# Nearest-neighbour upsampling by two: each store's copy shared between VectorE and ScalarE

## The chip, the cores and the metric

The kernel runs on one core of a Trainium2 chip. The metric is the device time of one execution in microseconds; of a kernel the median of its runs is given.

A core has several engines with instruction queues of their own. Three matter here: VectorE (DVE in the profile) and ScalarE (ACT), which can copy data within the on-chip memory, and SyncE (SP), which issues DMA transfers. ScalarE can issue DMA transfers too, so there are two DMA queues, one fed by SP (q1 in the profile) and one by ScalarE (q10). Both are served by the core's 16 DMA engines.

## What is computed

```python
def setup_inputs():
    batch, channels, h, w = (16, 64, 64, 64)
    return {'x': np.random.randn(batch, channels, h, w).astype(np.float32), 'scale_factor': 2}

def reference(x, scale_factor):
    ...
    for i in range(new_h):
        for j in range(new_w):
            result[:, :, i, j] = x[:, :, i // scale_factor, j // scale_factor]
    return result
```

The input is 16 x 64 images of 64 x 64 float32, 16.78 MB. Each element goes to a 2 x 2 block of the output, so the output is four times as large, 67.11 MB. There is no arithmetic.

## The kernel before

All 65536 image rows are laid over 128 partitions, R = 512 rows of 64 elements for each. A row becomes two output rows of 128 elements, 256 elements in all, and the 256 elements lie next to each other in the output. So a partition's part of the output is one contiguous stretch, and a store of k rows writes k x 1024 bytes for each partition.

Everything on the chip lives in one tile, `mem`. Its upper part, `xt`, from element WF = 79 x 256 = 20224 on, takes the whole input, 512 x 64 elements. The part below is free space for expanded rows. Three loads on SP bring the input: rows 0 to 31, 32 to 287 and 288 to 511 (`HEAD`, `cuts`, L192 to L195). They are issued ahead of the barrier at the start of the program (`begin_before_barrier`).

Then nine steps follow, n = 0 to 8, with 54, 38, 54, 60, 54, 62, 64, 62 and 64 rows (`rows`, L181). In a step a copy expands k rows into a region `u` of `mem` and a store sends the region to the output. The copy's source is `expanded(r0, r1)` (L197), the rows of `xt` with each row repeated twice and each element repeated twice. The regions alternate. Even steps use the bottom of `mem`, from element 0. Odd steps use the stretch that ends where the rows of this step begin, `at = WF + r0 * W - size`; so they overwrite input rows that earlier steps have already expanded. A copy must wait until the store that last used any of its elements has landed, which in most steps is the store two steps before.

All copies run on VectorE. In step 0 there are two, one for row 0 (L214), which needs the first load alone, and one for the other 53 (L215). The other steps have one each. The stores of steps 0, 1 and 8 are issued by SP, and those of steps 2 to 7 by ScalarE, whose queue holds nothing else. At the end `close_early` arranges that all engines but SP and GpSimd are finished early, and that SP's last instruction waits for the last store alone.

Below, "copy n" and "store n" are those of step n.

Of the kernel before, what the change touches and what calls it, by code (L numbers as in the profile page):

```python
# [153 lines left out]
@with_exitstack  # L154
def kernel(
    ctx: ExitStack,
    tc: tile.TileContext,
    x: bass.AP,
    scale_factor: int,
    out: bass.AP,  # L160
):
    nc = tc.nc
    nc.at_finalize(begin_before_barrier)
    nc.at_finalize(close_early)
    P = nc.NUM_PARTITIONS
    s = int(scale_factor)
    B, C, H, W = x.shape
    R = B * C * H // P
    fdt = x.dtype

    xp = x.rearrange("b c h w -> (b c h) w").rearrange("(p r) w -> p r w", p=P)
    op = out.rearrange("b c (h hd) w -> (b c h) (hd w)", hd=s).rearrange(
        "(p r) w -> p r w", p=P
    )

    rows = [54, 38, 54, 60, 54, 62, 64, 62, 64]  # L181
    GROW = s * s
    FREE = 79
    WF = FREE * GROW * W
    assert sum(rows) == R
    mem_pool = ctx.enter_context(tc.tile_pool(name="mem", bufs=1))
    mem = mem_pool.tile([P, WF + R * W], fdt, name="mem")
    xt = mem[:, WF:].rearrange("p (r w) -> p r w", r=R)

    HEAD = 32  # L192
    cuts = [0, HEAD, R // 2 + HEAD, R]
    for lo, hi in zip(cuts, cuts[1:]):
        nc.sync.dma_start(out=xt[:, lo:hi], in_=xp[:, lo:hi])  # L195

    def expanded(r0, r1):  # L197
        return (
            xt[:, r0:r1].unsqueeze(2).unsqueeze(4).to_broadcast([P, r1 - r0, s, W, s])
        )  # L200

    r0 = 0
    before = (0, 0)
    for n, k in enumerate(rows):
        size = k * GROW * W
        at = 0 if n % 2 == 0 else WF + r0 * W - size
        assert at >= before[1] or at + size <= before[0]
        before = (at, at + size)
        u = mem[:, at : at + size].rearrange(
            "p (k a w b) -> p k a w b", k=k, a=s, w=W  # L210
        )
        k0 = 1 if n == 0 else 0
        if k0:
            nc.vector.tensor_copy(out=u[:, :k0], in_=expanded(r0, r0 + k0))  # L214
        nc.vector.tensor_copy(out=u[:, k0:], in_=expanded(r0 + k0, r0 + k))  # L215
        issuer = nc.sync if n in (0, 1, len(rows) - 1) else nc.scalar
        issuer.dma_start(out=op[:, r0 : r0 + k, :], in_=u)
        r0 += k
# [35 lines left out]
```

## Time and profile before

| what | value |
|---|---|
| median of three runs | 197.15 us (197.02 to 197.16) |
| the profiled execution, its own time | 197.01 us |
| span in the profile, first to last instruction | 195.7 us |
| read from and written to HBM | 16.78 MB and 67.11 MB, 429 GB/s over the span |
| the three loads land at | 4.86, 24.2 and 41.1 us |
| store 0 issued, landed | 38.5, 57.5 us |
| store 8 issued, landed | 166.4, 195.7 us |
| issue of a store to its landing, least, median, most | 18.9, 26.5, 36.7 us |

The span is the time from the first to the last instruction that the profile shows; some 1.3 us of the execution lie around it. DVE is VectorE, ACT ScalarE, SP SyncE; ACTq and SPq are their DMA queues. L215 is line 215 of the kernel. A group such as `mem<-mem 128x13824` is a copy within `mem` of 13824 elements for each of 128 partitions; with 256 elements a row that is 54 rows. The time in brackets is how long the engine was idle before the instruction, with what ended the wait. The chain of waits is followed back from the last instruction, at each step to whatever released it; it names what came last at each point, not what else was under way.

### The profile page before, as it was taken

Reading aid. Unit: us, or ns where it says so; the run is one execution under the profiler, and the core shown is the slowest. Engines: PE = TensorE matmul, PEld = TensorE weight load, DVE = VectorE, ACT = ScalarE, POOL = GpSimd, SP = SyncE. Lnnn points to the kernel's source line nnn. Section 1 sums busy time; section 2 is a strip of 40 time slices with the busy share of each in tenths; the row PEclk is TensorE's granted clock in tenths of the full one; section 3 lists DMA queues with packets and bytes.
Section 4 is the critical chain, followed back from the end, with each engine's and each line's share of the span. In section 5 each row is a group of like instructions: output and inputs, shape, how many; then the busy total and the mean of one; then the engine's idle time right before and its main releaser. Section 6 shows DMA issues by size and latency. Waiting matters only on the chain.

```text
span 195.7 us, 76 instructions
## 1 busy us (share of the span) xinstructions
DVE 76.9 (39%) x10; POOL 0.2 (0%) x4
## 2 busy tenths in 40 slices
DVE  0000099990029287059008805920790079000000
POOL 0000000000000000000000000000000000000000
DMA  9999989989898988999999899999999999999994
GB/s 429 429 429 429 402 375 492 445 362 543 362 435 382 540 384 362 543 402 402 402 492 452 362 543 415 415 415 415 429 429 429 429 415 441 550 476 422 429 429 214
DMA packets 1728, 83.89 MB, mean 429 GB/s; under 512 B 192, under 2 KB 192, under 8 KB 192
## 3 DMA queue, kind: packets, MB, share of 16 engines
q10 hardware_dynamic: 864, 46.66, 55.0%
q1 hardware_dynamic: 864, 37.22, 44.3%
HBM read 16.78 MB, written 67.11 MB: 429 GB/s over the span
## 4 chain that ended last, share of the span: by engine, by line
DMA 61%; DVE 24%; SPq 0%; issue 0%
DMA out_dram<-mem 49%; DVE mem L215 24%; DMA mem<-in_x_dram 12%; SPq L195 0%
## 5 line engine op out<-in xcount | busy, mean ns | idle before, releaser
L215 DVE COPY mem<-mem 128x13824 f32<-128x13824 f32 (+5 forms) x9 | 76.6, 8515 | 84.6 <-DMA out_dram<-mem 65.5
L214 DVE COPY mem<-mem 128x256 f32<-128x256 f32 x1 | 0.3, 293 | 4.9 <-DMA mem<-in_x_dram 4.9
L235 POOL MEMSET const-bfloat16-1.0<- 128x1 bf16 x1 | 0.1, 101 | 0.0
L235 POOL MEMSET const-uint8-127<- 128x1 uint8 x1 | 0.1, 101 | 0.0
L235 POOL MEMSET const-float32-0.0<- 128x1 f32 x1 | 0.1, 98 | 0.2 <-issue 0.2
L235 POOL MEMSET const-float32-1.0<- 128x1 f32 x1 | 0.1, 98 | 0.0
## 6 DMA issues: line engine op xcount, KB each, us to landing
out_dram<-mem ACTq DMA_DIRECT2D x2, 7936.0 KB, 31.6
out_dram<-mem ACTq DMA_DIRECT2D x2, 6912.0 KB, 23.7
out_dram<-mem ACTq DMA_DIRECT2D x1, 7680.0 KB, 26.1
mem<-in_x_dram SPq DMA_DIRECT2D x1, 7168.0 KB, 40.2
out_dram<-mem SPq DMA_DIRECT2D x1, 6912.0 KB, 18.9
out_dram<-mem SPq DMA_DIRECT2D x1, 4864.0 KB, 25.1
mem<-in_x_dram SPq DMA_DIRECT2D x1, 1024.0 KB, 4.8
mem<-in_x_dram SPq DMA_DIRECT2D x1, 23.8
```

The lines of the kernel that those rows point to most:

```text
L214: nc.vector.tensor_copy(out=u[:, :k0], in_=expanded(r0, r0 + k0))
L215: nc.vector.tensor_copy(out=u[:, k0:], in_=expanded(r0 + k0, r0 + k))
L235: nc = _bacc.Bacc("TRN2", target_bir_lowering=False, num_devices=1)
```

## The change

Each step's copy is cut in two. VectorE takes the first `kv` rows and ScalarE the rest. `kv` is five eighths of the step's rows, rounded down to an even number; in step 0 it is all rows but the last. The separate copy of row 0 is gone. Which queue issues which store stays the same.

```diff
-        k0 = 1 if n == 0 else 0
-        if k0:
-            nc.vector.tensor_copy(out=u[:, :k0], in_=expanded(r0, r0 + k0))
-        nc.vector.tensor_copy(out=u[:, k0:], in_=expanded(r0 + k0, r0 + k))
+        kv = k - 1 if n == 0 else k * 5 // 8 & ~1
+        nc.vector.tensor_copy(out=u[:, :kv], in_=expanded(r0, r0 + kv))
+        nc.scalar.copy(out=u[:, kv:], in_=expanded(r0 + kv, r0 + k))
         issuer = nc.sync if n in (0, 1, len(rows) - 1) else nc.scalar
         issuer.dma_start(out=op[:, r0 : r0 + k, :], in_=u)
```

| step | 0 | 1 | 2 | 3 | 4 | 5 | 6 | 7 | 8 |
|---|---|---|---|---|---|---|---|---|---|
| rows | 54 | 38 | 54 | 60 | 54 | 62 | 64 | 62 | 64 |
| VectorE | 53 | 22 | 32 | 36 | 32 | 38 | 40 | 38 | 40 |
| ScalarE | 1 | 16 | 22 | 24 | 22 | 24 | 24 | 24 | 24 |

## The prediction

> **What bounds the kernel now.** I read the page first: what each engine is busy with, and how full the DMA engines are.
>
> ```profile
> span 195.7 us, 76 instructions
> ...
> DVE 76.9 (39%) x10; POOL 0.2 (0%) x4
> ...
> q10 hardware_dynamic: 864, 46.66, 55.0%
> q1 hardware_dynamic: 864, 37.22, 44.3%
> ...
> DMA 61%; DVE 24%; SPq 0%; issue 0%
> ```
>
> The two DMA queues fill 55.0 + 44.3 = 99.3% of the DMA engines' span. The last line, from the chain that ended last, tells another story: 24% of 195.7 us, some 47 us, goes to VectorE's copies, and the change speeds up just those. The two can't both be worth something, so the next view is the busy time by stretches, cut where one transfer's bytes end and the next one's begin. A cut lies about 0.8 us ahead of the landing (store 0 lands at 57.45, the cut is 56.62); for the columns, the first figures are the length of the stretch and VectorE's busy time in it, the last two the DMA engines' share and GB/s.
>
> ```profile
> 4.05:23.38 19.33, 0.29 (x1) 0.00 (x0) 1.00 1.01 436
> 23.38:40.30 16.92, 16.06 (x2) 0.00 (x0) 1.00 1.00 434
> 40.30:56.62 16.32, 3.46 (x1) 0.00 (x0) 1.00 1.00 434
> 56.62:68.10 11.48, 7.36 (x1) 0.00 (x0) 1.00 1.00 434
> 68.10:84.40 16.30, 8.16 (x1) 0.00 (x0) 1.00 1.00 434
> ...
> 156.85:168.55 11.70, 8.69 (x1) 0.00 (x0) 1.00 1.00 434
> 168.55:182.80 14.25, 0.00 (x0) 0.00 (x0) 1.00 1.00 435
> 182.80:195.30 12.50, 0.00 (x0) 0.00 (x0) 1.00 0.97 419
> ```
>
> From 4.05 us to the end every stretch runs at 434 to 436 GB/s, whether VectorE is busy for 95% of it (the second) or not at all (the seventh). The DMA engines have no gap that a faster copy could close. What the chain counts as VectorE's time is time in which another store was being drained: two regions are in use, and while one is refilled the other one's store runs. So the question is only how much slack each copy has, which the timeline gives (start, length, and in brackets the idle time ahead of it).
>
> ```profile
> 24.21 19.55 DVE L215 COPY mem<-mem 128x13568 f32<-128x13568 f32 x2 [19.05 <-DMA mem<-in_x_dram]
> 57.48 7.36 DVE L215 COPY mem<-mem 128x13824 f32<-128x13824 f32 x1 [13.72 <-DMA out_dram<-mem]
> 69.00 8.16 DVE L215 COPY mem<-mem 128x15360 f32<-128x15360 f32 x1 [4.17 <-DMA out_dram<-mem]
> 85.22 7.36 DVE L215 COPY mem<-mem 128x13824 f32<-128x13824 f32 x1 [8.05 <-DMA out_dram<-mem]
> ```
>
> The idle time in a copy's row is how long the copy before it had been done when the DMA engines were still busy with the older store: 4.17 us after copy 2, 8.05 after copy 3. A store must be issued about 1.0 us before its first byte moves (the first load is issued at 0.0, and the rate over 0 to 2 us stays at 0 until 1.0), so the time that copy n may take is from its start to the cut where store n's bytes begin, less 1.0. Copy 2: 57.48 to 68.10, less 1.0, is 9.6 us, of which it uses 7.36. Copy 3: 69.00 to 84.40, less 1.0, 14.4, uses 8.16. The later ones have 14 to 17 and use 7.4 to 8.7. Copy 0 alone is close: it ends at 38.51, and store 0's bytes begin at 40.30, so 40.30 - 1.0 - 38.51 = 0.8 us.
>
> **The change part by part.** VectorE's price comes from two forms: 16384 elements take 8.694 us and 9728 take 5.227, that is 0.521 ns an element and 0.16 us a piece.
>
> Copy 0. The early copy of one row (0.293 us at 4.86) goes; VectorE now takes rows 0 to 52 and ScalarE row 53. VectorE still has 53 rows, 13568 elements. That form took 14.286 us, 1.05 ns an element, twice the others; with the same shape I take the same time, from 24.21 to 38.50. If it ran like the rest (7.2 us) store 0 would only wait behind the last load in SP's queue until 40.30. ScalarE's row needs the load that lands at 24.19, then under 0.5 us. Store 0's issue on SP now waits for two engines; the semaphore step it may need took 17 to 28 ns there, covered by the 0.8 us. Without that cover it would cost itself, 0.03 us. Sum: 0.
>
> Copies 1 to 8. VectorE's parts are 22, 32, 36, 32, 38, 40, 38 and 40 rows of 256 elements; by the two-form price 3.1, 4.4, 5.0, 4.4, 5.2, 5.5, 5.2 and 5.5 us. ScalarE's are 16, 22, 24, 22, 24, 24, 24 and 24 rows. No row shows a ScalarE copy. The nearest are VectorE's: 0.521 ns an element from below, 1.14 (293 ns for 256) from above. I take 1.05, the slow form, since nothing says that ScalarE gets the fast one: 4.5 us for 16 rows, 6.1 for 22, 6.6 for 24. So a copy is done after 6.1 to 6.6 us in place of 7.4 to 8.7, and stores 2 to 8 are issued 1.3 to 2.1 us earlier (by the lower end, where VectorE's part decides, 2.9 to 3.2). All of it goes into slack: a store issued earlier stands longer in a queue whose engines run at 434 GB/s. Sum: 0, at both ends.
>
> The Trainium skill, "ScalarE: Activation LUTs", section "What ACT_TABLE_LOAD costs", has a switch of function table at about 2.66 us and a copy at 186 ns and 0.833 ns an element, which speaks against using ScalarE for a few copies. By it 24 rows take 5.3 us, and the load, even if it stood between the landing at 24.19 and row 53, would be over by 27.3; the sum by it is the same.
>
> New waits. ScalarE runs copy n, the issue of store n (n from 2 to 7), copy n+1, in that order. While its copy n+1 waits for store n-1 to land, only the issue of store n+1 stands behind it, and that needs copy n+1 anyway. SP's issues 0, 1 and 8 wait for rows 1, 16 and 24 of ScalarE's. Across the engines: ScalarE's part of copy 1 overwrites input rows of copy 0, so it waits for VectorE until 38.5; copy 1 has from there to 56.62 - 1.0, 17 us. All later overwrites are of rows read by copies that were done before the previous store was issued.
>
> Two queues. Store 2 is issued at about 63.6 in place of 64.87, while store 1 is still running on SP's queue. Where queues overlap they share: store 7 took 36.7 us to land, the longest of all stores, since store 8 ran beside it. If they shared evenly from 63.6, store 1's last 5.4 us would take 10.8 and it would land at 74.4; copy 3 would end at 81.0, and store 2 has bytes until 84.40. Still no gap: 0.
>
> The sum: span 195.7 + 0, and 197.01 - 195.7 = 1.3 us around it, is 197.0 for an execution like the profiled one. The median of the runs, 197.15, lies 0.14 above that; my forecast for the median is 197.1.
>
> **The rivals.** Their times are counted from 197.1.
>
> Copying on two engines slows the DMA engines (slower). Place: the stretches in which ScalarE copies, 181 rows x 256 x 1.05 ns = 48.7 us. For it: nothing here shows both engines at work at once beside stores. Against it: VectorE's copies, with twice the elements per us, cost at most 436 - 434 = 2 GB/s, under 0.5%, which over 48.7 us would be 0.2. It decides from 0.4 us, a loss of 0.8%, up; at 3% it costs 1.5 us, 198.6. Chance 6%. The Trainium skill, "SBUF — State Buffer", section "Who interferes with whom", says that DMA never contends with a compute engine; by that rule the rival falls away and 197.1 stands. VectorE's rows agree; none shows ScalarE.
>
> ScalarE is far slower than I take it (slower). Place: copy 2, with the least room. Its 22 rows, 5632 elements, use up the 9.6 us at (9.6 - 0.16) / 5632 = 1.68 ns an element. At 2.1, twice the slow form, copy 2 takes 12.0 us, store 2 comes 2.4 late: 199.5. Copies of 24 rows would then take 13.1 of 14.4 and still fit. Against it: no form in the trace is above 1.14. Chance 4%.
>
> The copies do not run side by side, because one engine's part waits for the other's. Then a copy takes 4.4 + 6.1 = 10.5 us at copy 2, 0.9 over its room: 198.0 if that happens in copy 2, nothing in the others (5.5 + 6.6 = 12.1 of at least 14.4). The parts touch different elements of the tile, which speaks against. Chance 2% of this moving the time.
>
> The earlier stores do fill a gap (faster). All idle time of the DMA engines after 4.05 us is in the last stretch, 3% of 12.5 us = 0.4; before 4.05 no copy matters. At best 197.1 - 0.4 = 196.7. Chance 3%.
>
> **How the numbers follow.** The forecast, no change, has 85%. I call 0.2%, 0.4 us, the least that a measurement of this kernel can tell (its runs lie within 0.14 us). Slower: 6 + 4, and half of the 2, about 11%; faster 3%; same 86%, the forecast and the rest. The range goes down to 196.7, the gap rival at its best, and up to 197.6, a DMA loss of 1% over the 48.7 us; beyond lie the dear ends of the slower rivals, under 10%.
>
> **What the next profile would show.** Right: again 434 or more GB/s in every stretch; VectorE busy for about 53 us (53 rows at 14.3, the other 278 rows at 37.1, and 8 x 0.16), ScalarE for 25 to 49; idle times ahead of the copies longer by 1 to 3 us each; store 0 issued at 38.5. Wrong: a stretch under 430 GB/s with ScalarE busy (contention); a DMA share below 1 near 68 us (copy 2 late) or near 40 us (store 0 late); or a span whose end moved while its stretches did not.

## The result and the profile after

| kernel | median, us | lowest to highest | ratio to before, 95% interval |
|---|---|---|---|
| before | 197.15 | 197.02 to 197.19 | |
| changed | 201.84 | 201.73 to 201.91 | 1.0239 (1.0227 to 1.0250) |

The change costs 4.7 us, where no change was forecast. The page of the changed kernel, with the lines that answer to those shown of before (span, busy times, DMA queues, chain by engine):

```profile
span 200.4 us, 99 instructions
...
DVE 52.5 (26%) x9; ACT 41.6 (21%) x10; POOL 0.2 (0%) x4
...
q10 hardware_dynamic: 864, 46.66, 53.9%
q1 hardware_dynamic: 864, 37.22, 43.3%
...
DMA 65%; DVE 13%; ACT 5%; issue 0%; SPq 0%; DVEq 0%; ACTq 0%
```

The same packets and bytes go through the two queues, but they now fill 97.2% of the span in place of 99.3%. Of 200.4 us, the 2.1% that are missing are 4.2 us. So the engines that move the data stand still somewhere, and the stretches show where. Here they are cut around the places where the rate falls to nothing; the columns are length, busy time of DVE, ACT and POOL, the TensorE clock, the DMA share and GB/s.

```profile
4.15:84.48 80.33, 26.67 (x4) 14.21 (x4) 0.00 (x0) 1.00 1.00 433
84.48:86.06 1.58, 0.83 (x1) 0.90 (x1) 0.00 (x0) 1.00 0.01 0
86.06:120.61 34.55, 8.82 (x2) 9.30 (x2) 0.00 (x0) 1.00 1.00 432
120.61:122.10 1.49, 0.88 (x1) 0.92 (x1) 0.00 (x0) 1.00 0.11 43
122.10:160.26 38.16, 9.84 (x2) 9.70 (x2) 0.00 (x0) 1.00 1.00 431
160.26:161.70 1.44, 0.84 (x1) 0.91 (x1) 0.00 (x0) 1.00 0.11 44
161.70:199.90 38.20, 4.66 (x1) 4.41 (x1) 0.00 (x0) 1.00 1.00 431
```

There are three holes, 1.58 + 1.49 + 1.44 = 4.5 us, and between them the DMA engines are full. The span grew by 200.4 - 195.7 = 4.7; the holes are all of it but 0.2. (A window credits a packet wholly at its start, so the length of a hole depends by some 0.2 us on where it is cut.) Nothing happens in the first 84 us: the copies of steps 0 to 3 are shared too, and no hole comes of it.

What the issuing engine did just before each hole stands in ScalarE's timeline (start, length, the queue's issues as ACTq, the idle time before and what ended it):

```profile
72.96 5.31 ACT L214 COPY mem<-mem 128x6144 f32<-128x6144 f32 x1 [10.64 <-DMA out_dram<-mem]
85.16 4.89 ACT L214 COPY mem<-mem 128x5632 f32<-128x5632 f32 x1 [6.89 <-DMA out_dram<-mem]
85.22 5.19 ACTq L216 DMA_DIRECT2D out_dram<-mem  x2
```

and, further on in the same view,

```profile
121.18 5.31 ACT L214 COPY mem<-mem 128x6144 f32<-128x6144 f32 x1 [25.41 <-DMA out_dram<-mem]
...
121.26 5.88 ACTq L216 DMA_DIRECT2D out_dram<-mem  x2
...
160.79 5.31 ACT L214 COPY mem<-mem 128x6144 f32<-128x6144 f32 x1 [28.30 <-DMA out_dram<-mem]
160.85 0.34 ACTq L216 DMA_DIRECT2D out_dram<-mem  x1
```

ScalarE's part of copy 3 (6144 elements at 72.96) is done at 78.27, and VectorE's at 78.02, but store 3 is not issued then. The next thing in ScalarE's queue is its part of copy 4 (5632 elements), which waits until store 2 has landed, at 85.1. Only behind it come the issues of stores 3 and 4 ("x2"). The first of them does not wait for the copy's end: it goes out at 85.22, 0.06 us after the copy's start. What holds it is the copy's wait. Store 2 was the last work the DMA engines had, so from its end they wait for its landing to be signalled, for the copy to start, for the issue, and for the first bytes of store 3. The same happens at 121 (store 5 behind copy 6) and at 160 (store 7 behind copy 8). The kernel is written with each issue ahead of the next step's copy; the order of an engine's queue is settled when the program is built, and it came out otherwise.

### The profile page after: what moved, and what is told of

It reads as the page before. It is cut to its first block, busy times and chain, and to the rows that moved or that the text cites. A ratio compares the mean times of both kernels' runs of the same rounds, so it can differ in the third digit from the quotient of the medians.

```text
span 200.4 us, 99 instructions
## 1 busy us (share of the span) xinstructions
DVE 52.5 (26%) x9; ACT 41.6 (21%) x10; POOL 0.2 (0%) x4
## 4 chain that ended last, share of the span: by engine, by line
DMA 65%; DVE 13%; ACT 5%; issue 0%; SPq 0%; DVEq 0%; ACTq 0%
DMA out_dram<-mem 53%; DVE mem L213 13%; DMA mem<-in_x_dram 12%; ACT mem L214 5%; SPq L195 0%; DVEq L213 0%; ACTq L216 0%; SPq L216 0%
## 5 line engine op out<-in xcount | busy, mean ns | idle before, releaser
L213 DVE COPY mem<-mem 128x8192 f32<-128x8192 f32 (+5 forms) x9 | 52.5, 5847 | 113.8 <-DMA out_dram<-mem 89.6
L214 ACT COPY mem<-mem 128x6144 f32<-128x6144 f32 (+3 forms) x9 | 40.3, 4483 | 122.7 <-DMA out_dram<-mem 86.5
## 6 DMA issues: line engine op xcount, KB each, us to landing
mem<-in_x_dram SPq DMA_DIRECT2D x1, 7168.0 KB, 40.2
```

The lines of the kernel that those rows point to most:

```text
L213: nc.vector.tensor_copy(out=u[:, :kv], in_=expanded(r0, r0 + kv))
L214: nc.scalar.copy(out=u[:, kv:], in_=expanded(r0 + kv, r0 + k))
```

## The experiments

The theory to be tested is that of the held issue: a hole comes where an issue stands behind a copy that waits for the store under way. The main rival is the prediction's own, contention: copying on two engines slows the DMA engines. Another is that any copy in the issuing queue delays its issues.

**Written order.** A step at the end of the build puts ScalarE's queue in the order in which the kernel is written. No copy changes.

```diff
...
+    for n, issue in enumerate(issues):
+        if which is None or n in which:
+            queue.remove(issue)
+            behind = [m for m, i in enumerate(queue) if number(i) > number(issue)]
+            queue.insert(behind[0] if behind else len(queue), issue)
...
```

> The changed kernel with one difference: in ScalarE's queue the issues of stores 3, 5 and 7 stand ahead of ScalarE's parts of copies 4, 6 and 8, as the kernel is written. Nothing else moves. Order theory (an issue stands behind a copy that waits for the older store, so the DMA engines run dry three times, about 1.55 us each): no gap at 84, 120 and 160 us, 197.1 to 197.4. Rival, contention (copies on two engines at once slow the DMA engines): the time stays at 201.8. Rival, any copy in ScalarE's queue delays each issue: stays near 201.8 too.

Measured: 197.19 us against 197.20 of before, ratio 0.9998 (0.9988 to 1.0008). ScalarE's timeline of this run, for the same place:

```profile
73.06 5.31 ACT L235 COPY mem<-mem 128x6144 f32<-128x6144 f32 x1 [10.68 <-DMA out_dram<-mem]
78.41 0.34 ACTq L237 DMA_DIRECT2D out_dram<-mem  x1
85.31 4.88 ACT L235 COPY mem<-mem 128x5632 f32<-128x5632 f32 x1 [6.93 <-DMA out_dram<-mem]
90.22 0.34 ACTq L237 DMA_DIRECT2D out_dram<-mem  x1
```

and its DMA queues:

```profile
q10 hardware_dynamic: 864, 46.66, 55.0%
q1 hardware_dynamic: 864, 37.22, 44.2%
```

Store 3 is issued at 78.41, 0.04 us after its copy's end, and the queues are back at 99.2%. All copies have the lengths that they have in the changed kernel, so the whole loss was in the order, and both rivals fall.

**One of the three.** The same step, for store 3 alone (`which` is the second issue in ScalarE's queue).

> The changed kernel with the issue of store 3 alone put ahead of copy 4; stores 5 and 7 stay behind copies 6 and 8. Order theory: the gap near 84 us goes, the two near 119 and 159 us stay: 201.8 less one third of 4.7, 200.3. Contention: 201.8.

Measured: 200.34 us, ratio 1.0153 (1.0135 to 1.0171). The hole near 84 us is gone, and two are left:

```profile
84.30:118.66 34.36, 9.65 (x2) 10.20 (x2) 0.00 (x0) 1.00 0.99 430
118.66:120.68 2.02, 0.87 (x1) 0.92 (x1) 0.00 (x0) 1.00 0.00 0
...
158.85:160.44 1.59, 0.84 (x1) 0.91 (x1) 0.00 (x0) 1.00 0.10 40
```

The one issue that was put back brings back 1.5 us of the 4.7, about a third.

**The wait without the copy.** The kernel before, with one more instruction in ScalarE's queue ahead of each of the issues of stores 3, 5 and 7; it waits until store 2, 4 or 6, the one before, has landed. ScalarE copies nothing.

```diff
...
+    for n in held:
+        u, value = lands[stores[n - 1].name]
+        s = stores[n]
+        hold = mybir.InstEventSemaphore(
...
+                        wait_mode="sem-ge-imm",
+                        wait_value=value,
...
+        kept.insert([i.name for i in kept].index(s.name), hold)
```

> The kernel before, all copies on VectorE and no ScalarE copy at all; ScalarE's queue gets a wait ahead of the issues of stores 3, 5 and 7, each until the store before it has landed (the moment at which the issue happens in the changed kernel). Order theory: the same three gaps of about 1.55 us, 201.6 to 201.9. Contention: 197.1, since ScalarE copies nothing.

Measured: 201.73 us, ratio 1.0227 (1.0206 to 1.0249), span 200.4 as in the changed kernel. The stretches of the three holes (here without an ACT column, since ScalarE has nothing to show):

```profile
84.31:86.17 1.86, 0.89 (x1) 0.00 (x0) 1.00 0.08 33
120.71:122.16 1.45, 0.90 (x1) 0.00 (x0) 1.00 0.11 44
160.32:161.73 1.41, 0.88 (x1) 0.00 (x0) 1.00 0.01 0
```

The wait by itself makes the whole loss. Sharing the copies has no part in it.

**Two rows for ScalarE.** The changed kernel with a small share for ScalarE.

```diff
-        kv = k - 1 if n == 0 else k * 5 // 8 & ~1
+        kv = k - 1 if n == 0 else k - 2
```

> The changed kernel with ScalarE's share cut to one row of step 0 and two rows of each other step, 17 of 512 rows in place of 181. With these lengths the program's order has a single issue behind a later copy, that of store 5 behind copy 6. Order theory: one gap near 118 us, 197.15 + 1.55 = 198.7. Contention, in proportion to ScalarE's rows: 197.15 + 4.7 x 17 / 181 = 197.6.

Measured: 197.00 us, ratio 0.9992 (0.9982 to 1.0002): neither the one hole that I expected nor the 0.4 us of contention. The issue of store 5 does stand behind copy 6 in this queue, but the timeline of ScalarE shows what that copy waited for:

```profile
103.37 0.62 ACT L214 COPY mem<-mem 128x512 f32<-128x512 f32 x1 [9.99 <-DMA out_dram<-mem]
...
111.66 16.89 ACTq L216 DMA_DIRECT2D out_dram<-mem  x2
```

The two rows of copy 6 are elements 15872 to 16383 of the tile. Store 4's region ends at 13824, so they do not wait for store 4 at all, only for store 3, whose region does reach them. Store 3 landed at 103.3, copy 6's rows were out of the way at 104.0, and store 5 was issued at 111.66, when VectorE had done its part (103.41 + 8.16 = 111.57). An issue behind a later copy is harmless when that copy's wait ends early. My expectation had looked at the order alone. That other lengths of the copies gave another order of the queue is the second thing to see.

**Two rows, in the changed kernel's order.** The same share, with the issues of stores 3, 5 and 7 put behind copies 4, 6 and 8 by hand. This parts order from wait.

```diff
...
+    for store in (3, 5, 7):
+        n = queue.index(issues[store - 2])
+        queue[n], queue[n + 1] = queue[n + 1], queue[n]
...
```

> ScalarE's share cut to 17 of 512 rows as in the run with two rows, but ScalarE's queue put into the order of the changed kernel: the issues of stores 3, 5 and 7 behind copies 4, 6 and 8. The two rows of copies 4 and 8 lie where stores 2 and 6 read, those of copy 6 lie beyond store 4's region and wait for store 3 alone, which has landed by then. Theory that order alone costs: three gaps, 201.8. Theory that it is the wait for the store under way, ahead of the issue: two gaps of about 1.55 us, at 84 and near 159 us, 200.3. Contention in proportion to ScalarE's rows: 197.6.

Measured: 200.52 us, ratio 1.0172 (1.0156 to 1.0187). The stretches at the three places:

```profile
84.29:86.24 1.95, 0.93 (x1) 0.62 (x1) 0.00 (x0) 1.00 0.00 0
...
120.60:122.10 1.50, 0.69 (x1) 0.00 (x0) 0.00 (x0) 1.00 1.57 677
...
158.94:160.39 1.45, 0.91 (x1) 0.62 (x1) 0.00 (x0) 1.00 0.11 44
```

Holes at 84 and 159 us, 1.95 + 1.45 = 3.4, and none near 121 (a packet is credited at its start, so a short stretch can show a share over 1). It is the wait for the store under way that costs, and 17 rows of copying cost as much in such a place as the full share.

**Stores on SP.** The changed kernel, with every store issued by SP.

```diff
-        issuer = nc.sync if n in (0, 1, len(rows) - 1) else nc.scalar
+        issuer = nc.sync
```

> The changed kernel with stores 2 to 7 issued by SP instead of ScalarE, so that no copy stands in the queue that issues. Both copies stay as long as they are. Order theory: no gap, 197.1 to 197.3. If ScalarE's copying as such cost something beside stores, more than that.

Measured: 197.08 us, ratio 0.9997 (0.9988 to 1.0006). With the copies in one queue and the issues in another, no copy can stand ahead of an issue. This is the simple form of the change, and it is worth nothing: the DMA engines were the bound.

**Looking for a faster version.** Nearly all of the idle time that the DMA engines have in the kernel before is at its start: over the first 4.05 us their share is 0.76. Two loads of 256 rows replace the three, first in the kernel before, then in the changed kernel with written order.

```diff
-EARLY = 3
+EARLY = 2
...
-    HEAD = 32
-    cuts = [0, HEAD, R // 2 + HEAD, R]
+    cuts = [0, R // 2, R]
```

> The kernel before with two loads of 256 rows in place of three of 32, 256 and 224: the 1.05 MB of the first load take from 1.0 to about 4.0 us, 3.0 us, at the rate of the rest 2.4. If the small packets of the first load are what is slow, 0.4 to 0.7 us less, 196.4 to 196.8. If it is the start of any transfer, 197.15.

> The changed kernel with ScalarE's queue in written order and two loads of 256 rows. As with the two loads in the kernel before: 196.4 to 196.8 if the first load's small packets are slow, 197.15 if not. A difference between the two kernels with two loads would be what sharing the copies is worth when no issue is held.

Measured: 198.19 us, ratio 1.0055 (1.0043 to 1.0068), and 198.22, ratio 1.0056 (1.0043 to 1.0069). Both are slower, by 1.05 and 1.08 us, where I had expected a gain or nothing; sharing the copies again makes no difference between them. Store 0 was issued at 36.42 in the first of them, in place of 38.52. Two more runs ask whether that is the cause.

**Copy 0 in the short form**, in the kernel before, with its three loads; the early copy takes two rows, which leaves copy 0 with 52:

```diff
-        k0 = 1 if n == 0 else 0
+        k0 = 2 if n == 0 else 0
```

> The kernel before with the early copy of step 0 taking two rows, so that the other takes 52, an even number. If the long form (1.05 ns an element) came from the odd number of rows, copy 0 takes 7.1 us in place of 14.3 and store 0 is issued near 31.3, some 9 us before the last load's bytes end. The prediction's view (the store just waits behind the load in SP's queue): 197.15. Theory from the run with two loads (a store issued before the last load's last packets start makes these take 3.3 us in place of 2.4): 1.0 us more, 198.1.

**Two loads, store 0 late**: the kernel before with two loads, and in step 0

```diff
+        if n == 0:
+            nc.vector.tensor_copy(out=u[:, k - 7 :], in_=expanded(k - 7, k))
```

> The kernel with two loads, with one more copy in step 0: the last seven rows are copied a second time, about 2.0 us, so that store 0 is issued near 38.4, as in the kernel before. If the 1.05 us that two loads cost come from the early issue of store 0, they go: 197.1 to 197.2. If they come from the two loads themselves, 198.2.

Measured: with the short form 198.49, ratio 1.0067 (1.0050 to 1.0084); with two loads and store 0 issued late 197.21, ratio 0.9999 (0.9990 to 1.0008). With 52 rows in place of 53 copy 0 took 7.1 us, so the long form came with the odd number, and the store went out at 31.10. The page of before has the last load land 40.2 us after its issue, the DMA issues of the run with the short form 41.6:

```profile
mem<-in_x_dram SPq DMA_DIRECT2D x1, 7168.0 KB, 40.2
```

```profile
mem<-in_x_dram SPq DMA_DIRECT2D x1, 7168.0 KB, 41.6
```

So a store that is issued well before the last load is through delays that load, by about as much as the kernel loses (1.25 us of 197.24). The two loads themselves cost nothing and gain nothing. The last run asks whether it matters that the store follows the load in SP's queue.

**Copy 0 in the short form, store 0 on ScalarE's queue**: as the run with the short form, and

```diff
-        issuer = nc.sync if n in (0, 1, len(rows) - 1) else nc.scalar
+        issuer = nc.sync if n in (1, len(rows) - 1) else nc.scalar
```

> As the run with copy 0 in the short form, store 0 issued near 31 us, but by ScalarE's queue, so that it does not follow the last load in SP's. If the 1.25 us come from a store standing behind a load in one queue: 197.2. If they come from a store and a load running side by side at all: 198.5 or more, since here they share for longer.

Measured: 204.21 us, ratio 1.0360 (1.0343 to 1.0378). The stretches:

```profile
34.00:46.00 12.00, 2.33 (x1) 0.00 (x0) 1.00 0.94 353
46.00:69.70 23.70, 2.84 (x1) 0.00 (x0) 1.00 1.00 432
69.70:75.10 5.40, 5.37 (x2) 0.00 (x0) 1.00 0.03 10
```

From 34 to 46 us the engines move 353 GB/s, and 432 from there on. Not all of the slow stretch is load and store side by side. The trace keeps every packet with its start and length: on each of the 16 DMA engines the load's packet that starts near 34 us, just ahead of store 0's first, takes 3.6 us in place of 2.1, and no byte of the store moves before 37.4. In the stretch in which packets of both run, 38 to 46 us, each packet takes about 2.2 us in place of 2.0 to 2.1, together 404 GB/s. The same packets are the slow ones where store 0 stands behind the load in SP's queue: the last of the load on each engine takes 3.6 us with the short form and 3.3 in place of 2.4 with two loads, before the store's first packet there. Most of the 7.1 us lost here is another matter, a hole of 5.4 us by this window: store 0 shares first with the load and then with store 1, lands at 66.8 in place of 57.5, and copy 2, which waits for it, is late. No version beat the kernel before.

## Why the prediction was wrong

*What bounds the kernel* was right. Between the holes the DMA engines of the changed kernel run at 431 to 433 GB/s; stores on SP or in written order give 197.08 and 197.19 us. Two readings were off, and nothing hung on them. Of the stretches said to run at 434 to 436 the last shows 419, which the text itself counts later as 0.4 us of idle time. And not all later copies have room of 14 to 17 us: for copy 8 the same subtraction gives 168.55 - 157.66 - 1.0 = 9.9, though its store ran beside store 7 and had time.

*The price of the copies* was right or near. VectorE is busy for 52.5 us (53 said); ScalarE's copies take 40.3 us (25 to 49 said). I took 6.6 us for 24 rows from VectorE's slow form; they take 5.31. The Trainium skill, "ScalarE: Activation LUTs", section "What ACT_TABLE_LOAD costs", has 186 ns and 0.833 ns an element for an instruction with immediate scale and bias; an estimate by it is 5.30 us for 6144 elements, and the trace agrees. Of the 2.66 us that the section gives for a switch of table, the trace shows the load itself, 1.28 us at 1.74 us, long before the first copy.

*Two queues* was near. Store 1 shared with store 2 and landed near 73.0 (74.4 said for even sharing, 68.98 before), and no gap came from it.

*New waits* is the step that failed. It said that "ScalarE runs copy n, the issue of store n (n from 2 to 7), copy n+1, in that order", and drew from it that only the issue of store n+1 stands behind a waiting copy. In the changed kernel the issues of stores 3, 5 and 7 stood behind copies 4, 6 and 8. I had read the order from the kernel's text; before, with issues alone in ScalarE's queue, there had been nothing to get ahead of them, so the profile of before could not confirm it. It entered the sum with nothing. In its place the runs showed three holes, 4.5 us of the 4.7: the wait of copy 4, 6 or 8 for the store under way stood ahead of an issue that was ready. That wait alone, without any copy on ScalarE, costs as much (201.73); put back in the order of the text, the kernel takes 197.19, so the sum's other terms hold.

The right question was asked (what is queued behind a waiting instruction) but of one order alone. What the other order costs could have been worked out from before: a store issued only when the one before it has landed leaves the DMA engines idle from its last bytes to the next first ones, some 0.8 us from there to the landing and 1.0 from issue to first byte, 1.8 each time; the windows show 1.4 to 2.0. None of the rivals had this mechanism.

*The signs* named ahead could not tell it from contention. A stretch under 430 GB/s with ScalarE busy was to mean contention; all three holes look like that (ScalarE busy for 0.90 of 1.58 us in the first), and yet they are there without any copy on ScalarE. Busy times and the issue of store 0 came as said. VectorE's idle times did not grow by 1 to 3 us each: ahead of copy 3 it was 11.13 us in place of 4.17, since store 1 landed later, and ahead of copy 4 it fell from 8.05 to 7.21.

*Contention* falls: full shares on both engines run at 0.9998 and 0.9997 of the time before. That ScalarE would be too slow falls (0.86 ns an element), and so does one part of a copy waiting for the other: copy 2's parts start at 57.42 and 57.49.

*Copy 0.* It kept its long form and store 0 was issued at 38.62 (38.5 said). But the remark that in the short form "store 0 would only wait behind the last load in SP's queue" was wrong by 1.25 us.

## What to carry to other kernels

No transfer that is ready to be issued should stand in a queue behind a wait for the transfer under way. An engine may both wait and issue, as ScalarE does in written order at no loss; it is the order of the two that costs. Before copies are put on an issuing engine, read from the built program which issue ends up behind which wait; or let another queue issue. And where the DMA engines are full in every stretch, the engine time in the chain of waits is no promise of a gain: in written order VectorE's copies took 24 us less, 52.5 in place of 76.9, and nothing was gained.

## What was not expected of the hardware

A store can be issued too early. At 38.5 us, about 2 us ahead of the end of the last load's bytes, it costs nothing (197.21 with two loads); at 36.4 it costs 1.05 us and at 31.1 1.25 us, in the last of these with the last load landing 1.4 us later. It does not take the same queue: from ScalarE's queue store 0 slows the load as well. In each of these runs the slowing sits mainly in one packet of the load on each DMA engine, the one just ahead of the store's first packet there. Stores beside stores from two queues show nothing of the kind: stores 7 and 8 run together in the kernel before, at 435 GB/s from 168.55 to 182.80 us. What makes that packet slow was not found.

Not of the hardware but of the build: an engine's order as the program is built changes with the lengths of its copies: with two rows for ScalarE only store 5 was issued behind a later copy, with three eighths stores 3, 5 and 7.
